# Channel shuffle: fewer, larger DMAs with two buffers each, and all copies on VectorE

## The chip, the cores and the metric

The kernel runs on one core of a Trainium2 chip. The metric is device time in microseconds (us); lower is better. "Span" is the profiled time from the core's first to its last instruction; the measured time is 1.6 to 2.2 us over it.

## The reference

The channels of a pixel form 8 groups of 32; the kernel interleaves the groups. It is a pure move of 67.1 MB in and 67.1 MB out.

```python
x = np.random.randn(16, 64, 64, 256).astype(np.float32)      # groups = 8
x = x.reshape(batch, h, w, groups, channels_per_group)
x = x.transpose(0, 1, 2, 4, 3)
x = x.reshape(batch, h, w, c)
```

## The kernel before

32 tiles of 128 partitions x 16 KB (2.1 MB), five input and five output buffers. Loads are issued from SyncE, stores from ScalarE (two DMA queues); the copies that shuffle alternate between GpSimd and VectorE.

```python
in_pool = ctx.enter_context(tc.tile_pool(name="in_pool", bufs=_IN_BUFS))     # 5
out_pool = ctx.enter_context(tc.tile_pool(name="out_pool", bufs=_OUT_BUFS))  # 5
# ... cut ...
for t in range(ntiles):                                       # 32
    in_tile = in_pool.tile([P, free], mybir.dt.float32)       # free = 16 * 256
    nc.sync.dma_start(out=in_tile, in_=x_t[t])
    out_tile = out_pool.tile([P, free], mybir.dt.float32)
    src = in_tile.rearrange("p (i g j) -> p i j g", g=G, j=CPG)
    dst = out_tile.rearrange("p (i j g) -> p i j g", j=CPG, g=G)
    do_copy(copy_engines[t % len(copy_engines)], dst, src)    # "gv": GpSimd, VectorE
    nc.scalar.dma_start(out=out_t[t], in_=out_tile)
```

Of the kernel before, what the change touches and what calls it, by code (L numbers as in the profile page):

```python
# [2 lines left out]

# [4 lines left out]


_Q = int(os.environ.get("CS_Q", "16"))
_IN_BUFS = int(os.environ.get("CS_IN_BUFS", "5"))
_OUT_BUFS = int(os.environ.get("CS_OUT_BUFS", "5"))
_COPY_ENGINES = os.environ.get("CS_COPY_ENGINES", "gv")


@with_exitstack
def kernel(
    ctx: ExitStack,
    tc: tile.TileContext,  # L20
    x: bass.AP,
    groups: bass.AP,
    out: bass.AP,
):
    nc = tc.nc

    b, h, w, c = x.shape
    G = int(groups)
    CPG = c // G
    assert G * CPG == c, (c, G)  # L30

    P = nc.NUM_PARTITIONS

    n_pix = b * h * w
    assert n_pix % P == 0

    q = _Q
    pix_per_tile = P * q
    ntiles = n_pix // pix_per_tile
    assert ntiles * pix_per_tile == n_pix, (n_pix, pix_per_tile)  # L40

    free = q * c

    x_t = x.rearrange("b h w c -> (b h w c)").rearrange(
        "(t p f) -> t p f", p=P, f=free
    )
    out_t = out.rearrange("b h w c -> (b h w c)").rearrange(
        "(t p f) -> t p f", p=P, f=free
    )

    in_pool = ctx.enter_context(tc.tile_pool(name="in_pool", bufs=_IN_BUFS))
    out_pool = ctx.enter_context(tc.tile_pool(name="out_pool", bufs=_OUT_BUFS))

    eng_map = {"v": nc.vector, "g": nc.gpsimd, "s": nc.scalar}
    copy_engines = [eng_map[ch] for ch in _COPY_ENGINES]

    def do_copy(eng, dst, src):
        if eng is nc.scalar:
            eng.copy(out=dst, in_=src)
        else:  # L60
            eng.tensor_copy(out=dst, in_=src)  # L61

    for t in range(ntiles):
        in_tile = in_pool.tile([P, free], mybir.dt.float32)
        nc.sync.dma_start(out=in_tile, in_=x_t[t])  # L65

        out_tile = out_pool.tile([P, free], mybir.dt.float32)

        src = in_tile.rearrange("p (i g j) -> p i j g", g=G, j=CPG)
        dst = out_tile.rearrange("p (i j g) -> p i j g", j=CPG, g=G)  # L70
        do_copy(copy_engines[t % len(copy_engines)], dst, src)

        nc.scalar.dma_start(out=out_t[t], in_=out_tile)


# [1 line left out]
_INS = ['x', 'groups']  # L77
_OUTS = [((16, 64, 64, 256), 'float32')]
#: Inputs that are plain numbers.
_NUMBERS = {'groups': 8}  # L80


# [26 lines left out]
```

## Time and profile before

| | before |
|---|---|
| time, median (range) | 317.93 us (317.81 to 318.03, 3 runs) |
| span of the profile | 316.3 us |
| VectorE / GpSimd busy | 63.8 / 114.7 us |
| bytes moved | 134.22 MB, 424 GB/s over the span |

From the page of the kernel before: the engines' busy time, the DMA rows of the 40 slices of the span (tenths busy; GB/s), the chain that ended last, the two groups of copies (busy us, mean ns | idle before, who ended it), and the DMA issues (KB, us from issue to landing):

```profile
span 316.3 us, 247 instructions
...
DVE 63.8 (20%) x16; POOL 114.7 (36%) x20
...
DMA  7999999999999999999999999999999999999997
GB/s 290 431 402 431 431 431 431 431 431 433 431 431 431 431 431 431 431 431 431 431 431 431 431 431 431 431 431 431 431 431 431 431 431 431 431 431 431 433 431 332
DMA packets 9216, 134.22 MB, mean 424 GB/s; under 512 B 1024, under 2 KB 1024, under 8 KB 1024
...
DMA 94%; DVE 1%; SPq 0%; issue 0%; DVEq 0%
...
L61 POOL COPY out_tile<-in_tile 128x4096 f32<-128x4096 f32 x16 | 114.5, 7157 | 182.3 <-DMA in_tile<-in_x_dram 182.3
L61 DVE COPY out_tile<-in_tile 128x4096 f32<-128x4096 f32 x16 | 63.8, 3985 | 240.0 <-DMA in_tile<-in_x_dram 240.0
...
in_tile<-in_x_dram SPq DMA_DIRECT2D x32, 2048.0 KB, 38.8
out_dram<-out_tile ACTq DMA_DIRECT2D x32, 2048.0 KB, 25.3
```

The DMA is full from the second slice to the last but one. (A row is what a transfer moves for one partition, 16 KB here; a transfer lands when its completion is signalled.) Estimates from the measured 431 GB/s: a 2.1 MB transfer takes 4.9 us alone, 9.7 at half of it. A load lands 38.8 us after its issue, so four are in flight; a store after 25.3, so between two and three are. In the middle of the span both queues always hold work (in the DMA records, from 30 us to the last row of each, no 1.5 us pass without the start of a load row, or of a store row, on one of the 16 engines), so a copy that is late by a few us should not be noticed; `b_dve` below (ratio 1.0011) fits that.

### The profile page before, as it was taken

The page shows a single profiled execution, that of the slowest core. Times are in us where ns is not written, and L with a number is a line of the kernel's source. Part 1 is how long each engine was busy: PE and PEld are TensorE (multiplying, and loading weights), DVE is VectorE, ACT ScalarE, POOL GpSimd, SP SyncE. Part 2 cuts the span into 40 slices and gives each one's busy share as a digit, 9 for nine tenths or more (in the row PEclk, how much of TensorE's full clock was granted, in tenths as well). Part 3 has the DMA queues.
Part 4 walks back from the last instruction along what each step waited for, and adds up shares of the span by engine and source line. Part 5 has one row for each costly group of instructions (what it writes and reads, how often), then busy time and mean ns, then how long its engine had stood idle before and what let it go on. Part 6 is the DMA issues. An engine that isn't in the chain of part 4 may idle for free.

```text
span 316.3 us, 247 instructions
## 1 busy us (share of the span) xinstructions
DVE 63.8 (20%) x16; POOL 114.7 (36%) x20
## 2 busy tenths in 40 slices
DVE  0344004040130402204021040310404004040040
POOL 0863350803508044080530806217062260713500
DMA  7999999999999999999999999999999999999997
GB/s 290 431 402 431 431 431 431 431 431 433 431 431 431 431 431 431 431 431 431 431 431 431 431 431 431 431 431 431 431 431 431 431 431 431 431 431 431 433 431 332
DMA packets 9216, 134.22 MB, mean 424 GB/s; under 512 B 1024, under 2 KB 1024, under 8 KB 1024
## 3 DMA queue, kind: packets, MB, share of 16 engines
q1 hardware_dynamic: 4608, 67.11, 50.0%
q10 hardware_dynamic: 4608, 67.11, 49.5%
HBM read 67.11 MB, written 67.11 MB: 424 GB/s over the span
## 4 chain that ended last, share of the span: by engine, by line
DMA 94%; DVE 1%; SPq 0%; issue 0%; DVEq 0%
DMA in_tile<-in_x_dram 94%; DVE out_tile L61 1%; SPq L65 0%; DVEq L61 0%
## 5 line engine op out<-in xcount | busy, mean ns | idle before, releaser
L61 POOL COPY out_tile<-in_tile 128x4096 f32<-128x4096 f32 x16 | 114.5, 7157 | 182.3 <-DMA in_tile<-in_x_dram 182.3
L61 DVE COPY out_tile<-in_tile 128x4096 f32<-128x4096 f32 x16 | 63.8, 3985 | 240.0 <-DMA in_tile<-in_x_dram 240.0
L90 POOL MEMSET const-float32-0.0<- 128x1 f32 x1 | 0.1, 99 | 0.2 <-issue 0.2
L90 POOL MEMSET const-bfloat16-1.0<- 128x1 bf16 x1 | 0.1, 103 | 0.0
L90 POOL MEMSET const-uint8-127<- 128x1 uint8 x1 | 0.1, 103 | 0.0
L90 POOL MEMSET const-float32-1.0<- 128x1 f32 x1 | 0.1, 99 | 0.0
## 6 DMA issues: line engine op xcount, KB each, us to landing
in_tile<-in_x_dram SPq DMA_DIRECT2D x32, 2048.0 KB, 38.8
out_dram<-out_tile ACTq DMA_DIRECT2D x32, 2048.0 KB, 25.3
```

The source lines that it names most:

```text
L61: eng.tensor_copy(out=dst, in_=src)
L90: nc = _bacc.Bacc("TRN2", target_bir_lowering=False, num_devices=1)
```

## The change

The intent: larger transfers for less cost per row, and no GpSimd. A load is 8.4 MB (64 KB a partition), a store 4.2 MB (32 KB); a copy stays 16 KB. Each kind has only two buffers now, 192 KB a partition in all. (In the text on the runs, 4 MB and 8 MB stand for 4096 and 8192 KB, which are the 4.2 and 8.4 MB of here.) One load feeds four copies and two stores. The core of the diff, cut:

```diff
-_Q = int(os.environ.get("CS_Q", "16"))
-_IN_BUFS = int(os.environ.get("CS_IN_BUFS", "5"))
-_OUT_BUFS = int(os.environ.get("CS_OUT_BUFS", "5"))
-_COPY_ENGINES = os.environ.get("CS_COPY_ENGINES", "gv")
+_LOAD = 64
+_STORE = 32
+_COPY = 16
 ...
+    in_pool = ctx.enter_context(tc.tile_pool(name="in_pool", bufs=2))
+    out_pool = ctx.enter_context(tc.tile_pool(name="out_pool", bufs=2))
 ...
+    for q in loads:                                   # 8 x 64
+        in_tile = in_pool.tile([P, _LOAD * c], F32, name="in_tile")
+        nc.sync.dma_start(out=in_tile[:, : q * c], in_=src_rows)
+        for s in range(0, q, _STORE):
+            n = min(_STORE, q - s)
+            out_tile = out_pool.tile([P, _STORE * c], F32, name="out_tile")
+            for k in range(0, n, _COPY):
+                ...
+                nc.vector.tensor_copy(out=dst, in_=src)
+            nc.scalar.dma_start(
+                out=dst_rows[:, s * c : (s + n) * c], in_=out_tile[:, : n * c]
+            )
```

More of the change, by code (lines that the diff above doesn't have):

```diff
@@ L2 @@
-import os
 from contextlib import ExitStack
@@ L8 @@
 from concourse._compat import with_exitstack
-_Q = int(os.environ.get("CS_Q", "16"))
-_IN_BUFS = int(os.environ.get("CS_IN_BUFS", "5"))
-_OUT_BUFS = int(os.environ.get("CS_OUT_BUFS", "5"))
-_COPY_ENGINES = os.environ.get("CS_COPY_ENGINES", "gv")
+F32 = mybir.dt.float32
+P = 128
+_LOAD = 64
+_STORE = 32
+_COPY = 16
 @with_exitstack
@@ L29 @@
     CPG = c // G
-    assert G * CPG == c, (c, G)
-    P = nc.NUM_PARTITIONS
+    assert G * CPG == c
     n_pix = b * h * w
-    assert n_pix % P == 0
-    q = _Q
-    pix_per_tile = P * q
-    ntiles = n_pix // pix_per_tile
-    assert ntiles * pix_per_tile == n_pix, (n_pix, pix_per_tile)
-    free = q * c
-    x_t = x.rearrange("b h w c -> (b h w c)").rearrange(
-        "(t p f) -> t p f", p=P, f=free
-    )
-    out_t = out.rearrange("b h w c -> (b h w c)").rearrange(
-        "(t p f) -> t p f", p=P, f=free
-    )
@@ L51 @@
-    in_pool = ctx.enter_context(tc.tile_pool(name="in_pool", bufs=_IN_BUFS))
-    out_pool = ctx.enter_context(tc.tile_pool(name="out_pool", bufs=_OUT_BUFS))
-    eng_map = {"v": nc.vector, "g": nc.gpsimd, "s": nc.scalar}
-    copy_engines = [eng_map[ch] for ch in _COPY_ENGINES]
-    def do_copy(eng, dst, src):
-        if eng is nc.scalar:
-            eng.copy(out=dst, in_=src)
-        else:
-            eng.tensor_copy(out=dst, in_=src)
-    for t in range(ntiles):
-        in_tile = in_pool.tile([P, free], mybir.dt.float32)
-        nc.sync.dma_start(out=in_tile, in_=x_t[t])
-        out_tile = out_pool.tile([P, free], mybir.dt.float32)
-        src = in_tile.rearrange("p (i g j) -> p i j g", g=G, j=CPG)
-        dst = out_tile.rearrange("p (i j g) -> p i j g", j=CPG, g=G)
-        do_copy(copy_engines[t % len(copy_engines)], dst, src)
-        nc.scalar.dma_start(out=out_t[t], in_=out_tile)
+    x_flat = x.rearrange("b h w c -> (b h w c)")
@@ new lines, with rows @@
+    out_flat = out.rearrange("b h w c -> (b h w c)")
+    loads = [_LOAD] * (n_pix // (P * _LOAD))
+    assert sum(loads) * P == n_pix
+    in_pool = ctx.enter_context(tc.tile_pool(name="in_pool", bufs=2))
+    out_pool = ctx.enter_context(tc.tile_pool(name="out_pool", bufs=2))
+    def rows(flat, first, q):
+        return flat[first * c : (first + P * q) * c].rearrange("(p f) -> p f", p=P)
+    first = 0
+    for q in loads:
+        src_rows = rows(x_flat, first, q)
+        dst_rows = rows(out_flat, first, q)
+        in_tile = in_pool.tile([P, _LOAD * c], F32, name="in_tile")
[4 more added lines that the diff above has]
+            for k in range(0, n, _COPY):
+                m = min(_COPY, n - k)
+                src = in_tile[:, (s + k) * c : (s + k + m) * c].rearrange(
+                    "p (i g j) -> p i j g", g=G, j=CPG
+                )
+                dst = out_tile[:, k * c : (k + m) * c].rearrange(
+                    "p (i j g) -> p i j g", j=CPG, g=G
+                )
+                nc.vector.tensor_copy(out=dst, in_=src)
+            nc.scalar.dma_start(
+                out=dst_rows[:, s * c : (s + n) * c], in_=out_tile[:, : n * c]
+            )
+        first += P * q
```

## The prediction

With all terms the sum came to 317.0 us; 317.9 plus 0 to 2 of holes does not lead there, because a saving per row, which was subtracted, is cut.

> **What bounds the kernel now.** The DMA engines, end to end. The page's slices show them 90% busy or more in 38 of 40, at 431 GB/s in nearly all; the chain that ended last is 94% loads. [...] 134.22 MB at 431 GB/s are 311.4 us of the 316.3 us span. The other 4.9 us are lost in the first slice (290 GB/s: 2.6 us), the third (402: 0.5) and the last (332: 1.8). The copies hide: the groups show VectorE 20% and GpSimd 36% busy, and every idle stretch ended by a load. The time is 1.6 us over the span.
>
> **What the change does.**
> - Removed: 16 GpSimd copies of 7.1 us. Where the engines first overlap, the timeline has a VectorE copy at 5.79 us instead of 3.86. [...] Off the critical path: worth nothing.
> - Moved: all 32 copies to VectorE in the same shape, 3.87 us each, 124 us, 39% of the span.
> - DMA: 8 loads of 8.4 MB and 16 stores of 4.2 MB instead of 32 and 32 of 2.1; bytes equal. A 16 KB row holds its engine about 607 ns from start to start in the trace's DMA records[...]. [...]
> - Two buffers of each kind instead of five. This is the risk.
>
> **Is the DMA still fed?** Estimates from 431 GB/s and 3.87 us: a load takes 19.5 us alone, 38.9 at half rate beside stores; four copies 15.5; a store 9.7 alone, 19.5 at half rate. Load 0 lands near 22 us (now 8.5), with load 1 queued behind it, so the longer fill leaves no hole. Store 0 is issued near 30 us, store 1 and load 2 near 38. Then one load lands per 39 us, its successor issued 15 us earlier, and stores follow one another with 8 us of slack. The last load lands near 287 us with about one store outstanding; its first half is copied by 295, as that store ends, the second by 303, while a store runs. I expect no hole, or one or two of 1 to 2 us there.
>
> **Time.** 317.9[...], plus 0 to 2 of holes: 317.0 us, 8 in 10 between 315.3 and 321.0. Faster by over 2%: 0.02[...]; within 2%: 0.89; slower by over 2%: 0.09.
>
> **What would show it.** Right: no GpSimd copies; 32 VectorE copies of about 3.87 us; middle slices at 431 to 434 GB/s; none below 400 but the first, the last, perhaps one near 20 us and one near 295. The count of DMA packets tells whether rows were cut.
>
> **What would make it wrong.** The first store, queued behind loads, started 3.9 us after its issue; if that wait counts pieces, 64 KB pieces could make it 12 us or more, use up the slack and leave holes of 5 to 20 us. Copies above 4 us would leave a hole per store while stores run alone. A row pitch of 64 KB in HBM could be slower. Shares other than half and half would shift all landings.

## More of the kernel before

The experiments were made in four batches, on four chips of this kind; the kernel before had a median of 317.96 to 318.00 us in each batch.

Runs carry a state. For one core, "slow" only means over 1.5% above the fastest run of the same kernel.

## The result

| | before | changed |
|---|---|---|
| time, median (range) | 317.98 us (317.81 to 318.05, 4 runs) | 328.83 us (324.67 to 331.52, 4 runs) |
| fast runs | all | 324.67 and 327.46 |
| ratio of fast runs | | 1.0253, interval 1.0208 to 1.0297: slower |

A ratio is the mean time of one kernel's fast runs over that of the other's of the same rounds, so it is not quite the ratio of the medians quoted.

(The row of the kernel before has one run more than the table above.) The first profile of the changed kernel fell in a slow run (331.52 us). So I ran the same text again five times (label `a_again`; 324.73 to 329.68 us, four of them fast, ratio 1.0261, interval 1.0238 to 1.0284) and got the profile of a fast run, of 324.73 us. From its page, the lines that answer to those of before:

```profile
span 322.9 us, 133 instructions
...
DVE 121.9 (38%) x32; POOL 0.2 (0%) x4
...
DMA  9899899999999999999999999999999999999997
GB/s 390 390 414 495 308 430 471 398 430 430 442 402 390 442 414 438 394 390 446 410 442 390 390 451 418 430 390 394 446 430 422 386 390 451 438 414 446 394 455 325
DMA packets 3456, 134.22 MB, mean 416 GB/s; under 512 B 384, under 2 KB 384, under 8 KB 384
...
DMA 77%; DVE 18%; DVEq 1%; issue 0%
...
L62 DVE COPY out_tile<-in_tile 128x4096 f32<-128x4096 f32 x32 | 121.9, 3861 | 188.6 <-DMA out_dram<-out_tile 164.0
...
out_dram<-out_tile ACTq DMA_DIRECT2D x16, 4096.0 KB, 32.5
in_tile<-in_x_dram SPq DMA_DIRECT2D x8, 32.4
```

The count of DMA packets, 3456, is 24 transfers of 128 rows and 16 completion records each: rows of 64 and 32 KB were not cut. The slices still read as "9", so the DMA looks full; the GB/s row is what gives it away. It swings, partly because a 64 KB row is booked to the slice in which it starts (the window from 211 to 213 us reads a DMA share of 1.89); longer windows average that out. Windows of about one lap (one load and two stores, about 40 us), DMA share and GB/s last, first of before, then of the changed kernel:

```profile
core 0: us, DVE busy (x) POOL busy (x), PEclk, DMA share, GB/s
80.00:120.00 40.00, 7.72 (x2) 15.34 (x3) 1.00 1.00 430
120.00:160.00 40.00, 7.74 (x2) 15.34 (x3) 1.00 1.01 432
```

```profile
core 0: us, DVE busy (x) POOL busy (x), PEclk, DMA share, GB/s
80.00:120.00 40.00, 15.23 (x4) 0.00 (x0) 1.00 1.00 423
120.00:160.00 40.00, 15.28 (x4) 0.00 (x0) 1.00 0.99 416
160.00:200.00 40.00, 15.21 (x4) 0.00 (x0) 1.00 1.00 419
200.00:240.00 40.00, 15.29 (x4) 0.00 (x0) 1.00 1.00 419
```

About 3% is lost in every lap, while the share of busy time hardly moves: a row that takes longer (3960 ns instead of 2418, below) counts as busy for longer. And VectorE, which waited for loads before, now waits for stores (164.0 us), with 18% of the chain in copies instead of 1%: buffers have come onto the chain.

**What a lap looks like.** One lap of the changed kernel's timeline, from its fast profile (`a_again`) (start us, us, what, [idle before it, who ended it]; the issue lines merge several issues):

```profile
start us, us, engine line op out<-in xcount [idle before <-releaser]
162.78 7.60 DVE L62 COPY out_tile<-in_tile 128x4096 f32<-128x4096 f32 x2 [23.01 <-DMA out_dram<-out_tile]
170.41 40.57 SPq L50 DMA_DIRECT2D in_tile<-in_x_dram  x2
170.41 40.60 ACTq L63 DMA_DIRECT2D out_dram<-out_tile  x3
172.30 7.61 DVE L62 COPY out_tile<-in_tile 128x4096 f32<-128x4096 f32 x2 [1.92 <-DMA out_dram<-out_tile]
203.00 7.63 DVE L62 COPY out_tile<-in_tile 128x4096 f32<-128x4096 f32 x2 [23.09 <-DMA out_dram<-out_tile]
```

And one DMA engine's records around the restart, grouped from the trace's DMA records by fitting ends to starts (L a load row, S a store row, start in us, duration in ns in brackets; a 4-byte completion record is marked with a star):

```
changed: S157.15(1213) L158.36(2418) S160.77(1213) L*161.98 S*161.99 S161.99(1213) S163.20(1213)
         S164.41(1213) S165.62(1213) S166.83(1213) S168.04(1213) S169.25(1213) S170.46(1213)
         S*171.67 L171.67(3960) S175.63(1213) L176.84(2418)
before:  L100.02(611) S100.63(611) L101.24(611) S101.84(611) L102.45(611) S103.06(611)
```

Four things are to be seen here:

1. **The engine takes one row of each queue in turn, here of 64 and 32 KB, before of 16 and 16.** A load row of 64 KB is one piece of 2418 ns, a store row of 32 KB one of 1213 (before, both 611). So loads get two thirds, not half.
2. **Load and store end together.** A load is 8 rows an engine, and so is a store. Both land after 8 x (2.414 + 1.210) = 29.0 us of taking turns, here at 162.5 and 162.7. Only one store is left, 8 x 1.21 = 9.7 us.
3. **The next load must wait for that landing.** It needs the input tile that still lacks its last two copies, which need the output buffer that has just landed. From the end of the last engine's rows (162.1) it takes 0.7 us to the copy, 7.6 us of copying, and 1.0 us from issue to the first row (171.4): 9.3 us, against 9.7 of store. That is 0.4 us of slack.
4. **The first load row then takes 3960 ns instead of 2418**, with no other row moving on the engine: the store that was issued at the same time, 170.41, gets its turn after it. In the laps of this profile (from 91 us on) the slow rows are all such first rows; the second to eighth rows of each load took the usual time.

**The account.** I summed two things over the DMA records, each divided by the 16 engines. "Idle" is time in which an engine moved nothing, start and end of the kernel included. "Slow rows" is what load rows took beyond the usual time of their size (counted beyond 20 ns). "Rest" is the span less both: the rows at their usual pace. (Each figure was rounded by itself.)

| kernel | span | idle | slow rows | rest |
|---|---|---|---|---|
| before | 316.3 | 3.6 | 1.3 | 311.3 |
| changed, fast run (`a_again`) | 322.9 | 4.8 | 8.3 | 309.8 |
| changed, slow run | 329.7 | 10.7 | 9.1 | 309.9 |

The rest fell by 1.5 us: that is what the larger rows saved. Idle and slow rows took 8.1 us more even in the fast run. The slow run has nearly the same slow rows (0.8 us more) and 5.9 us more idle. In it, the engines ended the laps' loads with a spread of 2.5 to 3.1 us three times (at 124, 247 and 290 us), one to three engines being late, the last by about a 64 KB row; the others ran dry waiting for them. In the fast run that spread was 0.8 to 1.2 us in every lap from 122 us on. How the stragglers come about I did not test.

### The profile page after: what moved, and what is told of

Read it like the earlier page. It is cut to its first block, busy times and chain, and to the rows that moved or that the text cites. A ratio compares the mean times of both kernels' runs of the same rounds, so it can differ in the third digit from the quotient of the medians.

```text
span 329.7 us, 133 instructions
## 1 busy us (share of the span) xinstructions
DVE 122.4 (37%) x32; POOL 0.2 (0%) x4
## 2 busy tenths in 40 slices
DMA packets 3456, 134.22 MB, mean 407 GB/s; under 512 B 384, under 2 KB 384, under 8 KB 384
## 4 chain that ended last, share of the span: by engine, by line
DMA 77%; DVE 17%; DVEq 1%; issue 0%
DMA out_dram<-out_tile 71%; DVE out_tile L62 17%; DMA in_tile<-in_x_dram 7%; DVEq L97 1%; DVEq L62 0%
## 5 line engine op out<-in xcount | busy, mean ns | idle before, releaser
L62 DVE COPY out_tile<-in_tile 128x4096 f32<-128x4096 f32 x32 | 122.4, 3885 | 194.9 <-DMA out_dram<-out_tile 170.5
```

The source lines that it names most:

```text
L62: nc.vector.tensor_copy(out=dst, in_=src)
```

## The experiments

The theory after the result (L, lock step): unequal rows taken in turn, with two buffers, make both DMA queues run dry at once in every lap. Rivals: V, one copy engine instead of two is what costs; H, reads in rows of 64 KB at a pitch of 64 KB a partition, or loads of 8 MB as such, are slow; B, two buffers are too few, whatever the sizes.

All results are correct unless stated. Medians are of all runs, ratios of fast runs.

### b_dve: before, copies on VectorE alone

```diff
-_COPY_ENGINES = os.environ.get("CS_COPY_ENGINES", "gv")
+_COPY_ENGINES = os.environ.get("CS_COPY_ENGINES", "v")
```

> The kernel before with all 32 copies on VectorE; loads, stores and five buffers of each kind unchanged. Theory L (lock step: with two buffers of each kind and rows of 64 KB against 32 KB taken in turn, loads and stores run dry together, and the next load waits for the slowest engine and for the copies): copies are hidden behind five buffers, so 317 to 319 us, VectorE about 124 us busy. Rival V (one copy engine is what costs): 325 us or more.

Measured: 318.29 us (318.23 to 318.48), ratio 1.0011 (0.9998 to 1.0023), VectorE 123.9 us busy, middle slices at 430 to 437 GB/s. V falls: dropping GpSimd costs nothing by itself.

### a_again: the changed kernel once more

> The changed kernel once more, unedited, to see its spread and a second profile. Theory L: 324 to 332 us; every lap costs about 1.3 us of slow first load rows, and 0.3 us of idle DMA when the 16 engines end a load together, about 2 us more when one engine ends it a row of 2.4 us late; the number of laps with such a straggler should follow the time of the run. Rivals: no prediction of the spread.

Measured: 324.73, 326.11, 327.14, 327.14 and 329.68 us. The profile is shown above. A lap lasted 40.1 to 40.4 us from landing to landing, against 8 x (2.414 + 2 x 1.210) = 38.7 of rows.

### a_cut32: load rows cut into two of 32 KB

```diff
-        in_tile = in_pool.tile([P, _LOAD * c], F32, name="in_tile")
-        nc.sync.dma_start(out=in_tile[:, : q * c], in_=src_rows)
+        in_tile = in_pool.tile([P, 2, _LOAD // 2 * c + 16], F32, name="in_tile")
+        nc.sync.dma_start(
+            out=in_tile[:, :, : q // 2 * c],
+            in_=src_rows.rearrange("p (n f) -> p n f", n=2),
+        )
```

> The changed kernel with each 64 KB row of a load cut into two pieces of 32 KB (the input tile is padded by 64 bytes after each half, so that the rows are not contiguous in SBUF); same loads, stores, buffers, HBM addresses and waits. Theory L: loads and stores now take turns in equal pieces, a load lasts as long as two stores, the two queues do not run dry together: 315.5 to 319 us, no idle DMA before the last 40 us. Rival H (HBM reads with a pitch of 64 KB a partition, or loads of 8 MB as such, are slow): stays at 324 to 332 us. Rival V: stays at 324 to 332.

Measured: 317.79 and 320.34 us fast, four more between 322.70 and 323.21 slow; ratio 1.0034 (1.0003 to 1.0065). All HBM addresses, transfers and waits are those of the changed kernel, and the fast runs are within 1% of before: no run of the six is above 323.21 us, below all that H has: H falls. (`c_quarter` below, with the load rows whole, says so more strictly.) In the profile (span 320.9, a slow run) there is no idle between the start and 296 us, as L has it, and slow rows are down to 3.0 us. But the range that I gave was missed by most runs. Most of the loss in this profile is one hole of about 3.4 us at 296 us: the engines had drifted apart (the ends of one store were spread over 10.7 us), and the last copies waited for the slowest.

### a_twice: every copy made twice

```diff
                 nc.vector.tensor_copy(out=dst, in_=src)
+                nc.vector.tensor_copy(out=dst, in_=src)
```

> The changed kernel with every copy made twice (same result). Theory L: the copies between a landed store and the next load lie on the chain, 7.7 us more a lap and twice more at the end, of which little is hidden: 370 to 400 us. Rival H (transfers are slow, copies are hidden): below 340 us.

Measured: 385.21 us (384.02 to 387.44), ratio 1.2122. The slices of its page show one hole a lap:

```profile
GB/s 336 432 438 438 384 274 493 380 435 336 110 486 387 438 332 110 473 394 432 346 110 473 387 435 349 110 452 384 432 377 110 425 411 435 373 164 274 329 219 329
```

120 us more of VectorE work cost 58 us more than the changed kernel (385.21 less 327.14), although VectorE is busy only 63% of the span. The copies are on the chain.

### a_dve_act: half of the copies on ScalarE (it did not test what it was made for)

```diff
-                nc.vector.tensor_copy(out=dst, in_=src)
+                if k == 0:
+                    nc.vector.tensor_copy(out=dst, in_=src)
+                else:
+                    nc.scalar.copy(out=dst, in_=src)
```

> The changed kernel with the second of each pair of copies on ScalarE, so that the two copies of a store run side by side; loads, stores, buffers unchanged. Theory L: the gap from a landed store to the next load falls from 7.7 to about 4 us, well inside the 9.7 us that the other store still takes, so a straggling engine (2.5 to 3 us late) no longer leaves the DMA idle: no idle before the end, spread between runs below 2 us. What stays is the slow first rows of a load that starts on a dry load queue, 1.0 to 1.4 us a lap if they come from the load queue running dry: 320 to 324 us; 317 to 319 if they come from both queues being dry at once.

Measured: 338.45 us (338.14 to 338.63), ratio 1.0641. Two of my assumptions failed. A ScalarE copy took 7.2 us, not about 4, so a pair took 7.2 us, hardly less than two on VectorE (7.6). And ScalarE issues the stores, and its program had become two copies, then two issues:

```profile
94.45 7.20 ACT L65 COPY out_tile<-in_tile 128x4096 f32<-128x4096 f32 x1 [5.09 <-DMA out_dram<-out_tile]
94.49 3.98 DVE L63 COPY out_tile<-in_tile 128x4096 f32<-128x4096 f32 x1 [8.23 <-DMA out_dram<-out_tile]
124.42 7.19 ACT L65 COPY out_tile<-in_tile 128x4096 f32<-128x4096 f32 x1 [22.77 <-DMA out_dram<-out_tile]
124.48 7.51 ACTq L66 DMA_DIRECT2D out_dram<-out_tile  x2
```

The store whose copies ended at 101.65 is issued at 124.48, behind a copy that first waited for the other store. The run says nothing about L.

### a_load32x3 and a_load32x2: loads of 4 MB, three or two buffers of each kind

```diff
-_LOAD = 64
+_LOAD = 32
-    in_pool = ctx.enter_context(tc.tile_pool(name="in_pool", bufs=2))
-    out_pool = ctx.enter_context(tc.tile_pool(name="out_pool", bufs=2))
+    in_pool = ctx.enter_context(tc.tile_pool(name="in_pool", bufs=3))   # x2: stays 2
+    out_pool = ctx.enter_context(tc.tile_pool(name="out_pool", bufs=3)) # x2: stays 2
```

> Loads of 4 MB (32 KB a partition) in three buffers, stores of 4 MB in three; copies as in the changed kernel. Theory L: equal pieces, no lap in which both queues are dry, stragglers covered by the third buffer: 315.5 to 318 us, best of all so far; no load restarts, so slow rows only at the start.

> Loads of 4 MB in two buffers, stores of 4 MB in two: as the changed kernel but the load is half as large, so one load needs two copies, not four. Theory L: a load and a store end together, but the next load waits for two copies (7.7 us) while the other load and store need 19.4 us: the queues do not run dry: 316 to 319.5 us. Rival B (two buffers are too few, whatever the sizes): 323 us or more.

Measured: three of each 323.73 us (322.63 to 324.48), ratio 1.0177 (1.0156 to 1.0198); two of each 317.96 us (316.88 to 318.08), ratio 0.9991 (0.9978 to 1.0004). The second is as L has it, and B falls: two buffers of each kind are enough here if a load needs two copies, 7.7 us, while the other load and store need 19.4. The first contradicts me: with more buffers it is slower. Its profile has 5.5 us of slow rows though no queue ran dry in its middle, and the engines drift apart, from 0.6 to 5.5 us between the first and the last to end a load, with a hole of about 2 us near 309 us.

### c_in2out3 and c_in3out2: which third buffer

```diff
 _LOAD = 32
-... name="out_pool", bufs=2
+... name="out_pool", bufs=3        # c_in3out2: in_pool 3, out_pool 2
```

> Loads and stores of 4 MB, two input buffers, three output buffers. Tells which third buffer made three of each slower (323.7) than two of each (318.0). If the copies then wait for loads instead of stores and that alone brings the slow load rows: 321 to 325 us. If the third input buffer is at fault: 316.5 to 318.5.

> Loads and stores of 4 MB, three input buffers, two output buffers. If the third input buffer makes loads and stores drift apart between the engines: 321 to 325 us. If the third output buffer is at fault: 316.5 to 318.5, with the copies waiting for stores.

Measured: two in, three out 316.90 us (316.70 to 317.85), ratio 0.9972 (0.9959 to 0.9984); three in, two out 323.77 us (322.33 to 323.97), ratio 1.0172. It is the third input buffer. Lines of waits (us in total, times, longest) of the first and of the second:

```profile
DVE out_tile L62 <- DMA in_tile<-in_x_dram: 145.3, 13, 12.9
```

```profile
DVE out_tile L62 <- DMA out_dram<-out_tile: 172.5, 14, 13.6
```

Whether copies wait for loads or for stores does not decide it, then. With a third input buffer, slow rows (5.3 us) and drift (0.5 to 5.4 us) come back; with a third output buffer there are 1.6 us of slow rows, and the spread of the loads stays at 2.2. What slows load rows there, with rows waiting in both queues, is not settled.

### a_cut16: load rows cut into four of 16 KB

As `a_cut32`, with 4 for 2.

> As the run with loads cut into 32 KB, but cut into four of 16 KB, with stores of 32 KB a row. Theory L: the engines take one piece of each queue in turn, so stores now get two thirds while both run, loads run on without a break, and the only hole is at the end, some 1 to 5 us where the last stores wait for copies: 317 to 324 us. If the share did not follow the size of the pieces, loads and stores would each get half.

Measured: 327.44 us (327.31 to 327.73), ratio 1.0298, outside the range that I gave. The turns are as expected. With load rows of 0.607 us in turn with store rows of 1.210, the 8 store rows of an engine need 14.5 us (half and half would be 19.4). In the DMA records, the first two stores follow one another without a gap, and their completions are 14.55 us apart (50.03 and 64.58 us on the first engine to end; the later pairs 14.5 to 15.2). With equal rows, in `a_load32x2`, stores end 19.36 us apart. The 64.0 us that the page has from issue to landing of a load tell nothing here: they include the wait behind the load before it. The hole at the end is larger than I thought, 7.4 us from 297.4 to 304.8 us, because one engine ended the last load 12.4 us after the first. Small load rows were no remedy here.

### c_32x2_twice: loads of 4 MB in two buffers, every copy twice

> Loads and stores of 4 MB in two buffers each, every copy made twice. Theory L: 15.5 us of copies still fit into the 19.4 us that a load and a store take together, so the laps stay full; about 8 us are lost near 21 us, where the first stores start, and about 8 us at the end: 325 to 335 us, against 385 for the same doubling in the changed kernel.

Measured: 338.62 us (337.82 to 339.10), ratio 1.0654, above my range. The holes at the start (7.3 us) and the end (7.7) are there, and the laps have almost no idle, but slow rows grew to 6.5 us, for which I have no cause. The doubling cost 20.7 us here and 58 in the changed kernel: the slack of a lap is real.

### c_half and c_quarter: shorter copies (wrong results on purpose)

```diff
+    outs = [out_pool.tile([P, _STORE * c], F32, name=f"out_tile{i}") for i in range(2)]
+    for o in outs:
+        nc.vector.memset(o, 0.0)
 ...
-                nc.vector.tensor_copy(out=dst, in_=src)
+                half = m // 2                                  # c_quarter: m // 4
+                nc.vector.tensor_copy(out=dst[:, :half], in_=src[:, :half])
```

Everything else is the changed kernel: rows, transfers, two buffers, waits.

> The changed kernel with every copy cut to the first half of its elements (wrong result on purpose; the two output tiles are fixed and cleared once during the first load). It replaces the failed attempt with ScalarE: the gap from a landed store to the next load falls from 7.7 to about 4 us, while the other store still takes 9.7. Theory L: no idle DMA in the laps, stragglers or not, total idle about that of the kernel before (3.6 us), spread of the runs below 2 us; what remains is the first row of each load after the load queue ran dry, 1.0 to 1.5 us a lap: 321 to 324 us. If that row is slow only because both queues were dry: 317 to 319. Rival H: unchanged, 324 to 332.

> As the run with half copies, with a quarter of the elements (about 1.1 us a copy; wrong result on purpose). The load then starts some 2 us earlier, with 3 to 5 us of the other store still to go on every engine. Reading R1 (a load's first row is slow only where the store queue is dry too, so that nothing covers its start): slow rows fall to about those of the kernel before, 1 to 2.5 us in all, DMA idle about 4 us: 315.5 to 318.5 us, and no run above 320. Reading R2 (a load's first row is slow whenever the load queue ran dry): slow rows stay at 6 to 8 us, 320 to 323 us.

Measured, half: 322.44 us (320.53 to 324.06), ratio 1.0134 (1.0103 to 1.0164); the outputs are wrong, as meant. Idle between 30 and 300 us is 0.8 us, but the spread of the runs, 3.5 us, is larger than I expected, and 6.5 us of slow rows remain. They come in steps: the load that restarted at 88.9 us, with a store still running on every engine, had 0.02 us an engine; at 128.8 us 0.45; at 167.8, 207.2 and 247.6 us, when the store had just ended on more and more engines, 1.0, 1.4 and 1.8. These sums hold two kinds. At 207.2 and 247.6 most of it lies in the first row of the load (1.0 and 1.3). At 128.8 and 167.8 the first rows add 0.1 or less, and the second and third rows are slow, with rows in both queues: what slows those stays open. So the time lies in the range I gave, but not wholly for the reason I gave; to that extent the hit was luck.

Measured, quarter: 317.63 us (317.12 to 317.72), ratio 0.9984 (0.9971 to 0.9998). Windows of its laps:

```profile
core 0: us, DVE busy (x) POOL busy (x), PEclk, DMA share, GB/s
80.00:120.00 40.00, 4.14 (x4) 0.00 (x0) 1.00 1.00 433
120.00:160.00 40.00, 4.26 (x5) 0.00 (x0) 1.00 1.00 434
160.00:200.00 40.00, 5.51 (x6) 0.00 (x0) 1.00 1.00 433
```

The load queue still runs dry in every lap (no load row starts from 152.2 to 165.5 us, for one), loads still get two thirds, rows are still 64 KB, there are still two buffers. But the load is back before the store has ended, and slow rows fall to 1.9 us, with none of note after 31 us. So a dry load queue costs next to nothing here as long as the other queue has some us of rows left: R2 falls, and the run is as R1 has it. What the changed kernel lost is the stretch in which both queues are dry: idle, then a first row with no other row beside it, 1.0 to 1.4 us longer than usual on average in a lap.

The accounts of all profiles, computed as above (us):

| kernel | state | span | idle | slow rows | rest |
|---|---|---|---|---|---|
| b_dve | fast | 316.7 | 4.0 | 1.4 | 311.3 |
| c_quarter | fast | 315.5 | 4.0 | 1.9 | 309.5 |
| c_half | fast | 321.9 | 5.6 | 6.5 | 309.8 |
| a_twice | fast | 382.6 | 63.0 | 9.7 | 309.9 |
| a_cut32 | slow | 320.9 | 7.5 | 3.0 | 310.4 |
| a_cut16 | fast | 325.5 | 11.1 | 3.2 | 311.2 |
| a_load32x2 | fast | 315.9 | 4.0 | 1.8 | 310.0 |
| c_in2out3 | fast | 315.3 | 3.6 | 1.6 | 310.0 |
| a_load32x3 | fast | 322.7 | 6.6 | 5.5 | 310.6 |
| c_in3out2 | fast | 322.1 | 6.2 | 5.3 | 310.6 |
| c_32x2_twice | fast | 336.1 | 19.0 | 6.5 | 310.5 |

(`a_dve_act` is left out: its store rows were slow too, by 3.9 us.) The rest lies between 309.5 and 311.3 us in these accounts: 311.3 with load and store rows of 16 KB, 310.0 to 310.6 with 32 and 32, 309.5 to 309.9 with 64 and 32. Everything else is idle and slow rows. Only the account of the changed kernel was split into first and later rows; in `a_load32x3`, `c_in3out2`, `c_32x2_twice` and part of `c_half` the slow rows are not explained.

## Why the prediction was wrong

- **"The DMA engines, end to end" bind before; GpSimd is "off the critical path: worth nothing".** Right: `b_dve` is the same within 0.2%. All 32 VectorE copies took about 3.87 us, as predicted.
- **A saving per row (cut from the prediction above).** Its size was the author's estimate, worked out from a figure that no trace of this case shows. Measured: the rows went as single pieces (3456 packets), and the rest fell from 311.3 to 309.8 us.
- **"A load takes ... 38.9 at half rate beside stores", "its successor issued 15 us earlier", "stores follow one another with 8 us of slack".** This is the step that failed. I shared the engines by bytes; they took turns by rows, and a load row (2418 ns) was twice a store row (1213). A load took 29.0 us of turns, not 38.9, and landed with the store that its successor had to wait for. The successor was issued about 8 us after that landing, not 15 us before it, and the slack was 0.4 us, not 8. The prediction listed "shares other than half and half" among its doubts, but gave them no size.
- **"I expect no hole, or one or two of 1 to 2 us."** The term for holes was mis-sized: 0 to 2 us in the prediction, 8.1 us more of idle and slow rows in the fast profile and 14.9 in the slow one (10.7 + 9.1 against 3.6 + 1.3). I had also left out that the first row after a dry stretch is slow, 1.0 to 1.4 us a lap, which is the larger part in the fast run.
- **"Two buffers of each kind ... is the risk."** Half right. Two buffers with equal rows and loads of 4 MB lose nothing (`a_load32x2`, ratio 0.9991). It was two buffers together with a load that needs both output buffers in turn, and with unequal rows, which made that load land with the store: with equal rows `a_cut32` kept both and had no idle before 296 us.
- **"The first store, queued behind loads, started 3.9 us after its issue; if that wait counts pieces ... holes of 5 to 20 us."** Stores did start late (35 us, issued at 30.4), but load rows filled that time: no idle there.

Shown by experiments: the copy gap is on the chain (`a_twice`, `c_half`), and closing it removes the loss with transfers, rows, buffers and waits kept (`c_quarter`, 317.63 us); row sizes in turn decided each queue's share (`a_cut16`, 14.55 us for a store; `a_load32x2`, 19.36); neither the copy engine (`b_dve`, ratio 1.0011), nor HBM addresses (`c_quarter`, 0.9984), nor the number of buffers by itself (`a_load32x2`, 0.9991) is the cause. Open: what slows load rows with a third input buffer and the later rows in `c_half`, why the engines drift apart in some kernels, and what makes the stragglers of the slow runs.

The best version is `c_in2out3`, loads and stores of 4 MB in two and three buffers: 0.28% faster than before, with copies on VectorE alone. It keeps the saving per row (rest 310.0 us against 311.3) and none of the holes (idle 3.6 us, as before).

## What to carry to other kernels

Before you enlarge transfers, work out from the row sizes which DMA lands when, taking one row of each queue in turn as the records show it here, and follow the chain from a landed store through the copies to the next load: it should be shorter than what the other queue still holds, with some us to spare for a late engine. Here 9.3 us against 9.7 left 0.4, and in the slow run engines ended loads 2.5 to 3.1 us apart. With two buffers of each kind, equal rows and a load no larger than a store kept both queues full here (`a_load32x2`, 317.96 us, 4.0 us idle). A DMA row of "9"s in the slices hid 3% here (419 GB/s against 431); compare GB/s in windows of a lap.
